# Attention with the softmax division moved behind the values: one scaling of the output per head pair

## The chip, the cores and the metric

The kernel runs on one core of a Trainium2 chip. The metric is the device time of one execution in microseconds (us). A core has TensorE (PE in the profile, its weight loads PEld), VectorE (DVE), ScalarE (ACT), GpSimd (POOL) and SyncE (SP, which issues DMAs). Matrix products are written to banks of PSUM; POOL works on SBUF alone here.

## What is computed

The reference is a network of two blocks with many layers. The change touches one layer of it, the attention of the second block. Queries, keys and values come from one projection; queries and keys are normalised and rotated; 16 query heads of 64 numbers share 4 heads of keys and values; 512 tokens attend to 512 tokens without a mask:

```python
def attend_block(q_blk):
    scores = jnp.einsum('bkgqd,bksd->bkgqs', q_blk, kt).astype(jnp.float32)
    p = jax.nn.softmax(scores, axis=-1).astype(vt.dtype)
    return jnp.einsum('bkgqs,bksd->bkgqd', p, vt)
...
return o @ w_o
```

The softmax divides each row of exponentials by its sum. As the values are multiplied from the right, that division may be made before or after the product with them.

## The kernel before, in words

All activations lie with the features on the partitions and the 512 tokens along the free side. Products with float32 accuracy are made of two parts: `split` (line 284) makes a rounded high part `h` by a cast on ACT (line 288) and the rest `l` by a subtraction on DVE (line 289), and `acc3` (line 326) issues three matmuls per pair of operands: high by high (line 330), one low part by high (331) and the other (333).

`attention` (line 1191) first makes queries, keys and values, then walks through 16 heads `n`, two of which share a 128-partition tile `tl = n // 2` (e = n % 2). It works on four blocks of 128 queries per head:

- `score(n, b)` (line 1323): two matmuls (1327, 1328) of a query block with all keys into a bank of the group `pj` (three banks, named pj and pk); the row maximum on DVE (1330); the exponential on ACT with the sum of the row as a second result (1332), into a block `P` of 128 queries x 512 keys; the reciprocal of the sum on DVE (1333); the block times that reciprocal on POOL (1334). There are eight buffers for `P`, which is two heads, and six for the small tile `st` that holds maximum, sum and reciprocal.
- `values(n, sb)` (line 1337), for each of four blocks of 128 keys: four transposes on TensorE (1342) bring the four query blocks' columns into one bank of the tag `ps` (three banks), `split` makes `pth` and `ptl` of it, and `acc3` adds their products with the values to the pair's bank `pa_o` (two banks). All four key blocks of a head read all four of its `P`.
- When both heads of a pair are done, `split` makes the high and low part of the pair's output, `xh_oa` and `xl_oa`, from the bank.
- `finish_q` (line 1269), once per pair for the first five pairs, prepares a later query tile: one matmul (1264) that spreads a norm, a product on DVE (1266), two casts on ACT (1273) and two subtractions on POOL (1274).
- `half_proj` (line 306) is the output projection. Its first half needs the outputs of the first four pairs, and it is written behind the last two pairs.

In the program the scores of head n+1 stand block by block ahead of the values of head n. The order in which the instructions stand in each engine's queue is not written by hand: the program is built with a scheduler that simulates the engines' times (`schedule_with_timeline_sim=True`), and the engines then take their queues in that order.

The helper `rotated` (line 1228) already spreads per-token numbers over partitions in the way that the change uses: a copy and a subtraction of a few columns into a zeroed operand `rh` (high and low part, 1254), four matmuls with the identity (1257) that turn it round, a copy to SBUF on ACT (1259), and in `unit` a matmul with a selecting matrix `selb` (1264).

Of the kernel before, what the change touches and what calls it, by code (L numbers as in the profile page):

```python
# [9 lines left out]
F32 = mybir.dt.float32  # L10
F32R = mybir.dt.float32r
ACTF = mybir.ActivationFunctionType
ALU = mybir.AluOpType
# [3 lines left out]
S = 512  # L17
# [213 lines left out]
class Net:  # L231
# [959 lines left out]
    def attention(self, pool, nrm):  # L1191
        nc, a = self.nc, self.a
# [8 lines left out]
        selb = pool.tile([128, 4, 128], F32R, name="selb", tag="selb")  # L1201
# [67 lines left out]
        def finish_q(rr, tl):  # L1269
            t = unit(rr, tl % 4, qm[:, tl, :])  # L1270
            for e in range(2):
                f, g = halves[e], halves[1 - e]
                nc.scalar.copy(qs[e][f, tl, :], t[f])
                nc.gpsimd.tensor_sub(qs[e][g, tl, :], t[f], qs[e][f, tl, :].bitcast(F32))
# [43 lines left out]
        rqs = (rq, rq2)  # L1318
        self.load_exp(rq2[0:16, 0:1].bitcast(F32))

        oa, probs, outs = {}, {}, {}

        def score(n, b):
            tl, e = n // 2, n % 2
            qb = slice(128 * b, 128 * b + 128)
            p = self.bank("pj")
            nc.tensor.matmul(p, qs[e][:, tl, qb], ks[e][:, tl // 4, :], start=True, stop=False)
            nc.tensor.matmul(p, qs[e][:, tl, qb], kl[e][:, tl // 4, :], start=False, stop=True)
            st = self.tmp("st", [128, 4], bufs=6)
            nc.vector.tensor_reduce(st[:, 0:1], p, axis=mybir.AxisListType.X, op=ALU.max, negate=True)  # L1330
            pr = pool.tile([128, S], F32, name=f"P{n}{b}", tag="P", bufs=8)
            nc.scalar.activation(pr, p, ACTF.Exp, bias=st[:, 0:1], accum_out=st[:, 1:2])
            nc.vector.reciprocal(st[:, 2:3], st[:, 1:2])
            nc.gpsimd.tensor_scalar(pr, pr, st[:, 2:3], None, ALU.mult)
            probs[n, b] = pr

        def values(n, sb):
            tl, e = n // 2, n % 2
            sk = slice(128 * sb, 128 * sb + 128)
            p = self.bank("pt")  # L1340
            for b in range(4):
                nc.tensor.transpose(p[:, 128 * b:128 * b + 128], probs[n, b][:, sk], ident)
            self.nt += 1
            th = pool.tile([128, S], F32R, name=f"pth{self.nt}", tag="pth", bufs=4)
            tw = pool.tile([128, S], F32R, name=f"ptl{self.nt}", tag="ptl", bufs=4)
            self.split(th, tw, p)
            if n % 2 == sb == 0:
                outs[tl] = self.ps.tile([128, S], F32, name=f"pa_o{tl}", tag="pa", bufs=2)
            vs = slice(64 * e, 64 * e + 128)
            self.acc3(outs[tl], [(vh[:, sb, tl // 4, vs], vl[:, sb, tl // 4, vs], th, tw)],  # L1350
                      e == sb == 0, e == 1 and sb == 3)

        for b in range(4):
            score(0, b)
            if b:
                value(b)
        for n in range(16):
            tl = n // 2
            for b in range(4):
                if n < 15:  # L1360
                    score(n + 1, b)
                values(n, b)
                if (n % 2, b) == (1, 1) and tl + 3 < KD:
                    finish_q(rqs[(tl + 3) // 4], tl + 3)
            if n == 10:
                self.unspill_x(xs)
            if n % 2:
                oa[tl] = self.pair(f"oa{tl}")
                self.split(*oa[tl], outs[tl])
                if tl > 5:  # L1370
                    self.half_proj(a["wo"], oa, 0, (2 * (tl - 6),))
        self.half_proj(a["wo"], oa, 0, (4, 6))
# [252 lines left out]
```

## Time and profile before

| | |
|---|---|
| median of 3 runs | 3715.67 us (3714.78 to 3716.51) |
| the profiled execution | 3715.35 us |
| its span, first to last instruction | 3713.6 us |
| busy share of PE, PEld, DVE, ACT, POOL | 98%, 79%, 56%, 37%, 22% |
| mean granted clock of TensorE | 0.990 of 2.4 GHz |
| mean busy share of the 16 DMA engines | about a third |

Times in the rows are us from the span's start. Durations in the lists by line or tile are in ns. A matmul's shown duration is longer than the time that it keeps TensorE from the next one, as matmuls are pipelined: the distance between the starts of two that follow each other is what one costs. In a list, "idle before" is the time that the engine stood still ahead of such instructions, with what ended it behind the arrow. A line can be that of a helper: L288 and L289 are the cast and the subtraction of `split`, L330, L331 and L333 the matmuls of `acc3`.

### The profile page before, as it was taken

How to read it: one execution, taken by the hardware profiler on the slowest of the kernel's cores; microseconds unless marked ns; L12 is line 12 of the kernel's file. 1: busy time of each engine (PE TensorE's matmuls, PEld its weight loads, DVE VectorE, ACT ScalarE, POOL GpSimd, SP SyncE). 2: the span in 40 equal slices, each digit the busy share in tenths (PEclk: the TensorE clock that was granted, in tenths of full speed). 3: DMA queues.
4: the chain of work that ended last, by engine and by line, in shares of the span. 5: the costliest groups of instructions: out<-in, count | busy, mean ns of one | idle time of the engine just before them, and what ended most of it. 6: DMA issues, size and time to landing. Idle time of an engine off the chain costs nothing.

```text
span 3713.6 us, 45381 instructions
## 1 busy us (share of the span) xinstructions
PE 3636.4 (98%) x17516; PEld 2945.8 (79%) x17516; DVE 2070.6 (56%) x3210; ACT 1368.3 (37%) x2031; POOL 826.8 (22%) x649
## 2 busy tenths in 40 slices
PE   8999999999999999999999999989999999899998
PEld 6878778978888878878888888767788888688886
DVE  4354585863334344467784345576656464866463
ACT  4223453142223223363233233265444343444342
POOL 2112121421011102220441012585101012401011
PEclk9999998999999999999999999999999999999999
DMA  4233434422323233434332333301432324323332
GB/s 138 89 109 104 151 114 122 132 85 89 98 90 116 88 99 111 155 97 128 120 139 96 95 105 97 120 18 53 147 105 92 96 93 132 116 64 93 94 95 81
DMA packets 180032, 386.84 MB, mean 104 GB/s; under 512 B 40742, under 2 KB 83750, under 8 KB 178792
## 3 DMA queue, kind: packets, MB, share of 16 engines
q1 hardware_dynamic: 179816, 383.95, 33.0%
q8 instruction: 137, 2.24, 0.3%
q14 instruction: 79, 0.65, 0.1%
HBM read 350.85 MB, written 33.03 MB: 103 GB/s over the span
## 4 chain that ended last, share of the span: by engine, by line
PE 88%; DVE 5%; issue 3%; DMA 2%; ACT 1%; POOL 1%; SPq 0%; DVEq 0%; ACTq 0%; POOLq 0%
PE pj L331 11%; PE pj L330 11%; PE pj L336 8%; PE pk L330 6%; PE pk L331 6%; PE ps L330 4%; PE pa L330 4%; PE ps L331 4%; PE pa L331 4%; PE ps L336 4%; PE pa L336 4%; PE pk L336 4%; PE pj L333 3%; PE pk L333 2%; DVE wl L289 1%
## 5 line engine op out<-in xcount | busy, mean ns | idle before, releaser
L288 ACT CAST wh<-wr 128x1024 fp32r<-128x1024 f32 x612 | 590.6, 965 | 1203.1 <-PE pj L331 485.9
L289 DVE TENSOR_TENSOR wl<-wr,wh 128x1024 fp32r<-128x1024 f32 x610 | 695.5, 1141 | 500.1 <-PE pj L336 128.7
L515 POOL TENSOR_TENSOR t<-s,u 128x512 f32<-128x512 f32 x88 | 176.7, 2009 | 1054.9 <-DVE u L514 955.6
L330 PE MATMUL pj<-xh_ffn_norm,wh 128*128 128x512 f32 x856 | 339.1, 396 | 0.0
L331 PE MATMUL pj<-xl_ffn_norm,wh 128*128 128x512 f32 x856 | 338.8, 396 | 0.0
L336 PE MATMUL pj<-xh_ffn_norm,wl 128*128 128x512 f32 x856 | 217.7, 396 | 0.0
L375 POOL TENSOR_TENSOR ssq<-ssq,c 128x512 f32<-128x512 f32 x76 | 112.6, 1481 | 434.2 <-ACT c L372 430.1
L330 PEld LDWEIGHTS pj<-xh_ffn_norm,wh 128*128 128x128 f32 x856 | 160.9, 188 | 39.1 <-ACT wh L288 0.8
L331 PEld LDWEIGHTS pj<-xl_ffn_norm,wh 128*128 128x128 f32 x856 | 160.7, 188 | 39.0 <-DVE xl_ffn_norm L292 0.3
L336 PEld LDWEIGHTS pj<-xh_ffn_norm,wl 128*128 128x128 f32 x856 | 160.5, 188 | 38.7
L330 PE MATMUL pk<-xh_ffn_norm,wh 128*128 128x512 f32 x472 | 187.1, 396 | 0.3 <-ACT wh L288 0.2
L331 PE MATMUL pk<-xl_ffn_norm,wh 128*128 128x512 f32 x472 | 186.9, 396 | 0.0
L553 POOL TENSOR_TENSOR t<-t,s 128x512 f32<-128x512 f32 x44 | 57.2, 1299 | 570.1 <-DVE s L572 501.0
L288 ACT CAST hh_ffn_norm<-t 128x512 fp32r<-128x512 f32 x132 | 81.4, 618 | 276.8 <-POOL t L515 273.5
L289 DVE TENSOR_TENSOR hl_ffn_norm<-t,hh_ffn_norm 128x512 fp32r<-128x512 f32 x132 | 93.8, 711 | 145.3 <-ACT hh_ffn_norm L288 145.0
L330 PE MATMUL pj<-hh_ffn_norm,wh 128*128 128x512 f32 x396 | 157.0, 397 | 0.0
L331 PE MATMUL pj<-hl_ffn_norm,wh 128*128 128x512 f32 x396 | 156.9, 396 | 0.0
L330 PE MATMUL ps<-xh_ffn_norm,wh 128*128 128x512 f32 x384 | 152.7, 398 | 0.0
L330 PE MATMUL pa<-xh_ffn_norm,wh 128*128 128x512 f32 x384 | 152.4, 397 | 0.0
L331 PE MATMUL ps<-xl_ffn_norm,wh 128*128 128x512 f32 x384 | 151.9, 396 | 0.0
L331 PE MATMUL pa<-xl_ffn_norm,wh 128*128 128x512 f32 x384 | 151.9, 396 | 0.0
L336 PE MATMUL pk<-xh_ffn_norm,wl 128*128 128x512 f32 x472 | 120.0, 396 | 0.0
(800 smaller groups left out, 8432.6 us busy)
## 6 DMA issues: line engine op xcount, KB each, us to landing
wr<-in_cu SPq DMA_DIRECT2D x88, 512.0 KB, 3.5
wr<-in_win SPq DMA_DIRECT2D x56, 512.0 KB, 3.5
wr<-in_ffn2g SPq DMA_DIRECT2D x44, 512.0 KB, 3.4
wr<-in_ffn2u SPq DMA_DIRECT2D x44, 512.0 KB, 3.4
wr<-in_ffn1g SPq DMA_DIRECT2D x43, 512.0 KB, 3.4
wr<-in_ffn1u SPq DMA_DIRECT2D x43, 512.0 KB, 3.5
wr<-in_ffn1d SPq DMA_DIRECT2D x32, 512.0 KB, 3.5
wr<-in_ffn2d SPq DMA_DIRECT2D x32, 512.0 KB, 3.5
```

The costliest lines, as they stand in the source:

```text
L288: nc.scalar.copy(h, src)
L289: lo.tensor_sub(l, src, h.bitcast(F32))
L330: mm(out, sh, mh, start=first and i == 0, stop=False)
L331: mm(out, sh, ml, start=False, stop=False)
L333: mm(out, sl, mh, start=False, stop=last and i == n - 1)
L336: mm(out, sl, mh, start=False, stop=last and i == n - 1)
L375: (nc.gpsimd if k < n - 1 else nc.vector).tensor_add(ssq, ssq, sq)
L515: nc.gpsimd.tensor_mul(t, s, u)
L553: nc.gpsimd.tensor_mul(t, t, cs[1])
```

## The change

The exponentials go unscaled through the transposes and the product with the values. The sums of a pair's two heads are gathered in one small tile. Once per pair, `shares` takes the reciprocals, spreads them over the 64 partitions of each head with the matmuls of the helper above, and the pair's output is multiplied by the result before it is split.

```diff
-        oa, probs, outs = {}, {}, {}
+        oa, probs, outs, sums = {}, {}, {}, {}
+        rn = self.tmp("ssq", [128, 4, 128], F32R, bufs=1)
+        nc.gpsimd.tensor_scalar(rn, self.ones[:, None, :].to_broadcast([128, 4, 128]), 0.0, None, ALU.mult)
...
+            if e == b == 0:
+                sums[tl] = self.tmp("sm", [128, 4, 2], bufs=3)
             st = self.tmp("st", [128, 4], bufs=6)
             nc.vector.tensor_reduce(st[:, 0:1], p, axis=mybir.AxisListType.X, op=ALU.max, negate=True)
             pr = pool.tile([128, S], F32, name=f"P{n}{b}", tag="P", bufs=8)
-            nc.scalar.activation(pr, p, ACTF.Exp, bias=st[:, 0:1], accum_out=st[:, 1:2])
-            nc.vector.reciprocal(st[:, 2:3], st[:, 1:2])
-            nc.gpsimd.tensor_scalar(pr, pr, st[:, 2:3], None, ALU.mult)
+            nc.scalar.activation(pr, p, ACTF.Exp, bias=st[:, 0:1], accum_out=sums[tl][:, b, e:e + 1])
             probs[n, b] = pr
+
+        def shares(tl):
+            w = self.tmp("sw", [128, 4, 2], bufs=2)
+            nc.vector.reciprocal(w, sums[tl])
+            nc.vector.tensor_copy(rn[:, :, 0:2], w)
+            nc.vector.tensor_sub(rn[:, :, 8:10], w, rn[:, :, 0:2].bitcast(F32))
+            p = self.bank("pt")
+            for b in range(4):
+                nc.tensor.matmul(p[:, 128 * b:128 * b + 128], rn[:, b], self.identr, start=True, stop=True)
+            rs = pool.tile([128, S], F32R, name=f"rn{tl}", tag="rs", bufs=2)
+            nc.scalar.copy(rs, p)
+            p = self.bank("pt")
+            nc.tensor.matmul(p, selb[:, 0, :], rs, start=True, stop=True)
+            w = self.tmp("a")
+            nc.scalar.copy(w, p)
+            return w
...
             if n % 2:
                 oa[tl] = self.pair(f"oa{tl}")
-                self.split(*oa[tl], outs[tl])
+                t = self.tmp("t")
+                nc.vector.tensor_mul(t, outs[tl], shares(tl))
+                self.split(*oa[tl], t)
```

The bank group `pt` is the tag `ps`, the three banks of the transposes. The tag `ssq` has one buffer, which the norms ahead of and behind the attention use for their sum of squares.

## Rows read from the trace of the kernel before

**Rows 1.** The page: busy us, share of the span and instructions of each engine.
```profile
PE 3636.4 (98%) x17516; PEld 2945.8 (79%) x17516; DVE 2070.6 (56%) x3210; ACT 1368.3 (37%) x2031; POOL 826.8 (22%) x649
```
**Rows 2.** ACT's timeline, output casts of pairs one and six: start, us, instruction, idle before.
```profile
2462.82 0.58 ACT L288 CAST xh_oa<-pa_o 128x512 fp32r<-128x512 f32 x1 [1.44 <-PE pa_o L333]
...
2543.70 0.58 ACT L288 CAST xh_oa<-pa_o 128x512 fp32r<-128x512 f32 x1
```
**Rows 3.** Instructions of tiles xh_oa, P and ssq: ns min/median/max, first and last start.
```profile
L330 PE MATMUL pj<-xh_oa,wh x33: 390/396/496, 2548.9 to 2598.8; 128*128 128x512 f32 x33
...
L288 ACT CAST xh_oa<-pa_o x8: 575/586/588, 2462.8 to 2590.2; 128x512 fp32r<-128x512 f32 x8
L289 DVE TENSOR_TENSOR xl_oa<-pa_o,xh_oa x8: 690/690/692, 2463.4 to 2590.9; 128x512 fp32r<-128x512 f32 x8
...
L1342 PE MATMUL ps<-mats,P x256: 270/272/330, 2442.3 to 2583.4; 128*128 128x128 f32 x128
...
L369 ACT ACTIVATE ssq<-x x1: 617/617/617, 2596.5 to 2596.5; 128x512 f32<-128x512 f32 x1
```
**Rows 4.** Two stretches: length, busy of PE, PEld, DVE, ACT, POOL; clock, DMA, GB/s.
```profile
2458.90:2540.10 81.20, 72.97 (x365) 53.58 (x366) 61.21 (x130) 56.95 (x134) 74.66 (x50) 1.00 0.07 27
2548.80:2596.00 47.20, 47.20 (x229) 38.39 (x228) 27.53 (x49) 20.08 (x41) 11.42 (x8) 1.00 0.18 56
```
**Rows 5.** POOL's timeline ahead of the loop and over one pair of it.
```profile
2438.86 6.60 POOL L1334 TENSOR_SCALAR P<-P,st 128x512 f32<-128x512 f32 x4 [5.92 <-DVE st L1333]
...
2489.49 2.65 POOL L1274 TENSOR_TENSOR qs<-t,qs 64x512 fp32r<-64x512 f32 x2
2492.23 6.18 POOL L1334 TENSOR_SCALAR P<-P,st 128x512 f32<-128x512 f32 x4
2499.72 6.19 POOL L1334 TENSOR_SCALAR P<-P,st 128x512 f32<-128x512 f32 x4 [1.30 <-DVE st L1333]
2505.99 2.65 POOL L1274 TENSOR_TENSOR qs<-t,qs 64x512 fp32r<-64x512 f32 x2
```
**Rows 6.** PE's timeline around the end of one head.
```profile
2498.34 0.60 PE L1342 MATMUL ps<-mats,P 128*128 128x128 f32 x4
...
2499.70 0.39 PE L333 MATMUL pa_o<-pth,vl 128*128 128x512 f32 x1
2499.93 0.40 PE L1327 MATMUL pj<-ks,qs 128*128 128x512 f32 x1
...
2500.85 0.38 PE L1342 MATMUL ps<-mats,P 128*128 128x128 f32 x2
```
**Rows 7.** Groups by line, 2458.9 to 2540.1: busy us, mean ns, idle before with releasers.
```profile
L331 PE MATMUL pa_o<-ptl,vh 128*128 128x512 f32 x41 | 19.1, 466 | 2.8 <-DVE ptl L289 2.6
L1332 ACT ACTIVATE P<-pj,st 128x512 f32<-128x512 f32 x27 | 18.6, 690 | 12.3 <-DVE st L1330 6.6 <-PE ps L1342 5.7
...
L330 PE MATMUL pa_o<-pth,vh 128*128 128x512 f32 x40 | 17.1, 427 | 5.1 <-ACT pth L288 5.1
...
L1333 DVE RECIPROCAL st<-st 128x1 f32<-128x1 f32 x41 | 6.7, 162 | 12.1 <-ACT P L1332 11.7
```
**Rows 8.** ACT's timeline: an exponential that waited for transposes.
```profile
2498.65 0.69 ACT L1332 ACTIVATE P<-pj,st 128x512 f32<-128x512 f32 x1 [0.94 <-PE ps L1342]
```
**Rows 9.** Instructions like the added ones, by line or tile: ns min/median/max, first and last start.
```profile
L406 DVE CAST rth<-rtok x17: 161/169/594, 30.2 to 3699.9; 128x4 fp32r<-128x4 f32 x16, 128x2 fp32r<-128x2 f32 x1
...
L1266 DVE TENSOR_TENSOR t<-ps,qm x8: 690/691/692, 2415.5 to 2518.7; 128x512 f32<-128x512 f32 x8
...
L1259 ACT CAST rs<-ps x3: 585/585/586, 2377.6 to 2435.4; 128x512 fp32r<-128x512 f32 x3
```
**Rows 10.** PE's timeline: the four turning matmuls of a norm.
```profile
2377.05 0.56 PE L1257 MATMUL ps<-identr,rh 128*128 128x128 f32 x4
```
**Rows 11.** The page's groups: cast and subtraction of the same shape with SBUF sources.
```profile
L288 ACT CAST hh_ffn_norm<-t 128x512 fp32r<-128x512 f32 x132 | 81.4, 618 | 276.8 <-POOL t L515 273.5
L289 DVE TENSOR_TENSOR hl_ffn_norm<-t,hh_ffn_norm 128x512 fp32r<-128x512 f32 x132 | 93.8, 711 | 145.3 <-ACT hh_ffn_norm L288 145.0
```

## The prediction

> **What bounds the kernel now.** I read the page's busy shares first, then the busy time of the stretch that the change touches, then one engine after another in it, and last who waits for whom. Over the whole span TensorE is busy nearly all the time [rows 1], so time can only be won where TensorE has holes. The attention loop has them. Its eight head pairs are marked by the eight casts of the finished output; the first and the sixth lie at 2462.82 and 2543.70 [rows 2], so a pair takes 80.88/5 = 16.2 us. From about 2548.9 the output projection begins to fill TensorE [rows 3], and until 2596 it is busy for 47.20 of 47.20 us [rows 4]. There a saving on any other engine buys nothing, and each added matmul costs its full time.
>
> In the five pairs from 2458.9 to 2540.1 POOL is the fullest engine: 74.66 of 81.2 us, 14.9 per pair (TensorE's 72.97 overlaps its matmuls with each other); DVE has 61.21 (12.2), ACT 56.95 (11.4) [rows 4]. POOL's 14.9 are eight products of a probability block at 6.18/4 = 1.55 us and two subtractions that split the next query tile, 2.65 together [rows 5]. It stops only for about 1 us per pair, when it waits for a reciprocal.
>
> TensorE issues 365 matmuls there, 73 per pair: 40 of scores and values, one that spreads a norm, and 32 transposes. Successive 512-column ones start 0.23 us apart (2499.70, 2499.93); four transposes show 0.60 us of which the last has 0.27, so each costs 0.11 [rows 6]. That is 41 x 0.23 + 32 x 0.11 = 12.95 us of work in 16.2, or 3.2 us of holes per pair. Of these the trace names 5.1 + 2.8 us in five pairs as TensorE waiting for the cast and the subtraction that split a transposed block [rows 7], 1.6 per pair.
>
> **What does not fit a plain POOL bound.** No instruction is listed as waiting for POOL's product. Its run of four that starts at 2492.23 ends at 2498.41 [rows 5], and the transposes that follow on TensorE are at 2498.34 and 2500.85 [rows 6]. The four at 2498.34 are the last of the head before, since the exponential at 2498.65 waited for them to free its block [rows 8]; so the products lay ready for 2.4 us. TensorE takes its queue in order, and that order is laid out when the program is built, with POOL's step in it. A new order is laid out without it.
>
> **The change, part by part.**
>
> *Removed.* 64 POOL products leave: 8 x 1.55 = 12.4 of POOL's 14.9 us per pair. The 1.55 us between an exponential and its transposes go as well, and so does the queue in which the fourth block of a head waited for the three before it, about 6.2 us in all [rows 5]. The 41 reciprocals of one column, 6.7 us in five pairs [rows 7], give DVE back 1.3 per pair. The small statistics tile is free after the exponential instead of after POOL; eight probability blocks still hold two heads, so an exponential still waits for the transposes two heads back, 5.7 us in the five pairs for the blocks scored in pj alone [rows 7, 8].
>
> *Added, once per pair.* DVE: a reciprocal, a copy and a subtraction of eight columns. The nearest rows are 0.162 for one column [rows 7] and 0.169 for four [rows 9]; I take 0.165 each, bounds 0.14 and 0.2, together 0.5. One product of a PSUM bank and a 128x512 tile takes 0.69 [rows 9]. DVE goes from 12.2 to 12.2 - 1.3 + 1.2 = 12.1. ACT: two copies out of PSUM at 0.585 [rows 9], from 11.4 to 12.6. TensorE: four 128-column matmuls and one of 512. The same four as they stand in the norms show 0.56 us of which I give the last 0.27 as for the transposes [rows 6, 10], so 0.10 each, and 4 x 0.10 + 0.23 = 0.63 per pair; 13.6 us of work instead of 12.95. The cast and subtraction of the output now read SBUF instead of PSUM: 0.618 against 0.586 and 0.711 against 0.690 on the same shape [rows 3, 11], 0.05 per pair, off TensorE's path.
>
> *Added, once.* The zero fill of the 128x512 operand on POOL, 1.55 us as the product of that shape, bounds 1.3 (half of 2.65, on half the partitions) and 1.65 (6.60/4); POOL stands idle for 5.92 us just ahead of the loop [rows 5]. Taken at nothing; without that cover it would delay what POOL does for the queries by at most 1.65. The operand's place is wanted again by the square at 2596.5 [rows 3], thirteen us after the last transposes at 2583.4: nothing. The last pair's output gets a product of 0.69 ahead of its cast; the cast was at 2590.2 [rows 3], while TensorE was full with the other half of the projection: nothing, at most 0.7.
>
> *Queues and banks.* Each pair takes two more turns of the three PSUM banks that the transposes use, eleven instead of nine, and the product waits on DVE for the spread sums. Behind it in DVE's queue stand the maxima of the next scores, for which the exponentials wait. The sums are complete one head before the product needs them, so all five steps can be done early. I take no stall, and keep the stall as a rival.
>
> *The sum.* Without POOL the floor of a pair is TensorE's 13.6. I don't take the floor: the 1.6 us in which TensorE waits for cast and subtraction do not involve POOL, and I keep them, so 13.6 + 1.6 = 15.2, a gain of 1.0 per pair. From the first transpose at 2442.3 to 2548.9 [rows 3] there are 106.6/16.2 = 6.6 pairs: -6.6 us. In the other 1.4 pairs TensorE is full: +1.4 x 0.63 = +0.9. Net -5.7. Behind the loop TensorE's work is unchanged and starts that much earlier. The profiled execution took 3715.35 us (span 3713.6 and 1.75 around it); the median of the runs, 3715.67, is 0.3 above. I put the sum on the median: **3710.0**. Bounds of the pair: 13.6 (no holes) and 16.2 (no gain).
>
> **The rivals.**
>
> *The forecast (0.45).* Waits for the split blocks between 1.0 and 2.2 us per pair: -9.7 to -1.8, so 3706 to 3714.
>
> *The floor (0.25).* POOL was what placed the holes, all of them, and the new order closes them: 2.6 x 6.6 = 17.2 less 0.9, 3699.4; with up to 1.0 us of holes left per pair it is 3699.4 to 3706. For it: POOL is 92% busy in the stretch [rows 4], and where TensorE had other work at hand from 2548.8 on, it had no holes at all. Against it: the waits on cast and subtraction, and three banks that must now also carry the sums. The Trainium skill, page "Perfetto Trace Analysis", section "Identifying the Most-Contended Engine", says that the engine of highest occupancy is the one to relieve, and that TensorE's room is judged by its weight loads, not its matmuls. By that rule POOL alone is the limit here and this rival is the outcome; the trace agrees on the occupancy (weight loads 53.58 of 81.2 us [rows 4]), but not on the waits, where no one waits for POOL.
>
> *POOL was beside the path (0.18).* The products lay ready for 2.4 us, the cycle is transposes, cast, subtraction, block free, exponential, and the pair stays at 16.2 with the new work inside its holes. Only the full stretch pays: +0.9, 3716.6. This is the case in which the change does what it says and the time doesn't follow.
>
> *Slower: the spread sums stall TensorE (0.12).* The 512-column matmul of each pair stands in TensorE's queue behind the ACT copy of the four before it. If the order puts the two next to each other, TensorE waits at least that copy, 0.585, in every pair; with no gain elsewhere that is 8 x (0.63 + 0.585) = +9.7, 3725.4. It decides if the stall exceeds the 1.0 gained per pair. For it: the order is made with estimated durations, and DVE, ACT and TensorE alternate in five steps. Against it: the steps can start a head early, and the norms run the same pattern with the two matmuls apart.
>
> **How the numbers follow.** The forecast and the two cases with no or full gain carry 0.88. A range from 3700 to 3720 takes in the forecast, nearly all of the floor case, POOL beside the path, and the milder part of the stalls; about 0.15 is left out. The forecast's own range is 3706 to 3714. 0.2% of the time, about what a measurement of this kernel can tell from no change, is 7.4 us: faster means below 3708.2. The floor case gives 0.25 and a third of the forecast 0.15, so 0.40 faster; the rest of the forecast (0.30) and POOL beside the path (0.18) make 0.48 the same; the stalls 0.12 slower.
>
> **What the profile would show.** POOL should fall from 74.7 us to about 13 in five pairs; DVE stay at 12.1 per pair; ACT rise to 12.6; the distance between output casts be 15.2 in place of 16.2; matmuls per pair be 78. TensorE's waits for cast and subtraction should stay near 1.6 per pair: near zero means the floor case. Output casts still 16.2 apart mean POOL beside the path. A wait of the spreading matmul for an ACT copy, or of the product for one, in every pair means the stall. I am wrong in the mechanism if the pair shrinks while those waits grow, or if the time moves in stretches behind 2600 or ahead of 2440, where no work changes.

## The result, and the profile after

The changed kernel took **3692.86 us** (median of 4 runs, 3687.6 to 3693.97) against 3715.52 for the kernel before on the same chip (3714.78 to 3716.51): a ratio of 0.9934 [0.9923, 0.9946], or -22.7 us. The forecast was 3710.0, with a range down to 3700. The gain is four times the one forecast, so the question is where the other three quarters come from. The profiled execution took 3693.65 us, with a span of 3691.8.

The page's busy shares answer to [rows 1]. POOL has lost 95 us and TensorE only 9, of a span that is 22 shorter:

```profile
PE 3627.7 (98%) x17556; PEld 2952.2 (80%) x17556; DVE 2066.6 (56%) x3178; ACT 1375.5 (37%) x2047; POOL 732.1 (20%) x586
```

**The loop came out nearly as forecast.** ACT's timeline of the kernel after, the output casts of pairs one, two, five and six (to [rows 2]):

```profile
2452.63 0.69 ACT L288 CAST xh_oa<-t 128x512 fp32r<-128x512 f32 x1
2468.65 0.62 ACT L288 CAST xh_oa<-t 128x512 fp32r<-128x512 f32 x1
...
2514.37 0.62 ACT L288 CAST xh_oa<-t 128x512 fp32r<-128x512 f32 x1
2528.06 0.63 ACT L288 CAST xh_oa<-t 128x512 fp32r<-128x512 f32 x1
```

From the first to the sixth a pair takes 75.43/5 = 15.1 us, between the second and the fifth 45.72/3 = 15.24; forecast was 15.2, down from 16.2. The busy time of those three middle pairs and of the full stretch behind the loop, of the kernel after (length, busy of PE, PEld, DVE, ACT and POOL with their instructions, clock, DMA share, GB/s; to [rows 4]):

```profile
2468.65:2514.37 45.72, 44.45 (x236) 33.72 (x235) 36.71 (x67) 36.85 (x89) 7.67 (x6) 1.00 0.13 47
2532.40:2578.00 45.60, 45.60 (x225) 37.43 (x224) 28.04 (x47) 21.50 (x43) 0.00 (x0) 1.00 0.18 58
```

Per pair that is DVE 12.2 (forecast 12.1), ACT 12.3 (12.6) and POOL 2.6 (2.6). TensorE has 78 matmuls per pair; the 236 of the row include two at its edges. Behind the loop TensorE is still full.

**But most of the time moved where no work changed.** Four starts cut the span into stretches: the first projection of this layer, the first transposes of the loop, the first half of the output projection, the first projection of the next layer. The lists by tile of the kernel after (ns min/median/max, first and last start):

```profile
L330 PE MATMUL pj<-xh_attn_norm,wh x56: 389/395/498, 2329.9 to 2400.8; 128*128 128x512 f32 x56
...
L1360 PE MATMUL ps<-mats,P x256: 270/272/273, 2433.1 to 2560.9; 128*128 128x128 f32 x128
...
L330 PE MATMUL pj<-xh_oa,wh x40: 392/396/482, 2532.4 to 2590.3; 128*128 128x512 f32 x40
...
L330 PE MATMUL pj<-xh_xattn_norm,wh x72: 395/395/628, 2620.2 to 3227.9; 128*128 128x512 f32 x72
```

The two of them that [rows 3] lacks, of the kernel before:

```profile
L330 PE MATMUL pj<-xh_attn_norm,wh x56: 392/395/497, 2339.4 to 2410.2; 128*128 128x512 f32 x56
...
L330 PE MATMUL pj<-xh_xattn_norm,wh x72: 392/395/477, 2636.5 to 3246.5; 128*128 128x512 f32 x72
```

| stretch of the profiled execution, us | before | after | difference |
|---|---|---|---|
| start to the first transposes of the loop | 2442.3 | 2433.1 | -9.2 |
| to the first output projection | 106.6 | 99.3 | -7.3 |
| to the next layer's projection | 87.6 | 87.8 | +0.2 |
| to the end of the span | 1077.1 | 1071.6 | -5.5 |

The layer's own first matmul already starts 9.5 us earlier, 2329.9 against 2339.4, while the engines' queues up to there hold the same instructions in the same order, but for one: POOL's zero fill of 2.46 us. What differs is the pace of one kind of matmul. The lists by tile of `hl_ffn_norm`, an operand of the down-projections of all feed-forward layers, first of the kernel before, then of the kernel after:

```profile
L331 PE MATMUL pj<-hl_ffn_norm,wh x396: 388/397/402, 141.8 to 3678.4; 128*128 128x512 f32 x198
...
L331 PE MATMUL ps<-hl_ffn_norm,wh x264: 392/394/400, 149.6 to 3686.1; 128*128 128x512 f32 x132
...
L331 PE MATMUL pa<-hl_ffn_norm,wh x264: 391/394/400, 157.3 to 3693.8; 128*128 128x512 f32 x132
```

```profile
L331 PE MATMUL pj<-hl_ffn_norm,wh x396: 387/392/403, 141.5 to 3657.2; 128*128 128x512 f32 x198
...
L331 PE MATMUL ps<-hl_ffn_norm,wh x264: 387/389/399, 149.1 to 3664.7; 128*128 128x512 f32 x132
...
L331 PE MATMUL pa<-hl_ffn_norm,wh x264: 388/389/399, 156.6 to 3672.1; 128*128 128x512 f32 x132
```

The first product into `pj`, `ps` and `pa` are each 33 matmuls apart (11 blocks of features, three matmuls per block). So 66 matmuls take 157.3 - 141.8 = 15.5 us before, 0.235 each, and 156.6 - 141.5 = 15.1 after, 0.229 each. Taken over all starts that follow without a gap, a down-projection's 264 matmuls follow each other at 234.3 ns before and 229.0 after in six of the twelve stretches, at 233.4 and 226.8 in four, and at 233.3 and 233.4 in two. That is 6 x 264 x 5.3 + 4 x 264 x 6.6 ns = 8.4 + 7.0 = 15.4 us. The six and the two lie ahead of the attention, where 9.2 went, the four behind it, where 5.5 went; single executions differ by a few us in either. With the 7.1 of loop and output projection it makes 22.5 of the measured 22.7.

What can change the pace of a matmul whose queue is the same? The change's two new small tiles, `sm` (three buffers of 32 bytes per partition) and `sw` (two), belong to a pool of temporaries that stands for the whole program, and the tiles allocated behind that pool's space lie 160 bytes higher on every partition. In the built program `hh` and `hl` moved by that much; the weights `wh` and `wl` and the up-projections' operands `xh` and `xl` did not. (A matmul call of the program names its weights and, behind them, a second operand, called the moving operand below.)

### The profile page after: what moved, and what is told of

The parts are those of the page before. It is cut to its first block, busy times and chain, and to the rows that moved or that the text cites. A ratio compares the mean times of both kernels' runs of the same rounds, so it can differ in the third digit from the quotient of the medians.

```text
span 3691.8 us, 45267 instructions
## 1 busy us (share of the span) xinstructions
PE 3627.7 (98%) x17556; PEld 2952.2 (80%) x17556; DVE 2066.6 (56%) x3178; ACT 1375.5 (37%) x2047; POOL 732.1 (20%) x586
## 4 chain that ended last, share of the span: by engine, by line
PE 76%; DVE 4%; issue 3%; DMA 2%; POOL 1%; ACT 1%; SPq 0%; DVEq 0%; ACTq 0%; POOLq 0%
PE pj L331 10%; PE pj L330 10%; PE pj L336 7%; PE pk L330 5%; PE pk L331 5%; PE pa L330 4%; PE ps L330 4%; PE pa L331 4%; PE ps L331 4%; PE ps L336 3%; PE pa L336 3%; PE pk L336 3%; PE pj L333 3%; PE pk L333 2%; PE pj L725 1%
```

## The experiments

**The move alone (e1), and the change without the move (e2).** In e1 the kernel before gets the two tags and nothing else; in e2 the changed kernel takes its small tiles from tags that exist already:

```diff
 oa, probs, outs = {}, {}, {}
+nc.gpsimd.memset(self.tmp("sm", [128, 4, 2], bufs=3), 0.0)
+nc.gpsimd.memset(self.tmp("sw", [128, 4, 2], bufs=2), 0.0)
```
```diff
-sums[tl] = self.tmp("sm", [128, 4, 2], bufs=3)
+sums[tl] = self.tmp("rtok", [128, 4, 2], bufs=4)
-w = self.tmp("sw", [128, 4, 2], bufs=2)
+w = self.tmp("rv", [128, 4, 2], bufs=2)
```

> The kernel before with two zeroed small tiles of the change's sizes (three of 32 bytes, two of 32) and nothing else, so that every tile of the later pools starts 160 bytes higher, as after the change. Layout theory: the matmuls with the hidden activations hh and hl start 229.0 instead of 233.8 ns apart, about 3168 of them, so -15 us: 3700 to 3702, and the attention loop keeps its 16.2 us per pair. Rival (the gain came from the work that left, and the earlier start of the attention was that run's own): 3715.5, spacing 233.8.

> The change with its two small tiles put into buffers that exist already (the norms' 32-byte tiles), so that no other tile moves; the queues are those of the change. Layout theory: the loop's gain alone, -7 us: 3708 to 3709.5, pairs of 15.2 us, hh and hl matmuls 233.8 ns apart, attention starting when it did before. Rival: as the change, 3692.9.

e1 took 3700.26 us, a ratio of 0.996 [0.9945, 0.9975] to 3714.85 before: -14.6 us. e2 took 3706.3, 0.998 [0.9971, 0.999]: -8.6. The two add up to -23.1, against -22.7 of the change. The list by tile of e1, with TensorE's queue unchanged and two fills of 0.1 us on POOL added, shows the pace of the kernel after (66 matmuls in 157.9 - 142.8 = 15.1 us):

```profile
L331 PE MATMUL pj<-hl_ffn_norm,wh x396: 387/392/402, 142.8 to 3667.0; 128*128 128x512 f32 x198
...
L331 PE MATMUL ps<-hl_ffn_norm,wh x264: 387/389/399, 150.3 to 3674.4; 128*128 128x512 f32 x132
...
L331 PE MATMUL pa<-hl_ffn_norm,wh x264: 387/389/399, 157.9 to 3681.9; 128*128 128x512 f32 x132
```

In e2 the spacing is that of the kernel before, 66 matmuls in 155.6 - 140.1 = 15.5 us:

```profile
L331 PE MATMUL pj<-hl_ffn_norm,wh x396: 388/397/403, 140.1 to 3665.4; 128*128 128x512 f32 x198
...
L331 PE MATMUL pa<-hl_ffn_norm,wh x264: 391/394/400, 155.6 to 3680.8; 128*128 128x512 f32 x132
```

Its loop is that of the kernel after: the middle pairs are 15.24 us apart, and from the first transposes to the output projection it takes 99.4 us. So **the change as it was meant is worth -8.6 us, and two thirds of the measured gain is a side effect of where its tiles lie.** The profiled execution of e2 was the fastest of ten, 3701.88, and 5.7 us ahead of the kernel before by the time the loop begins, at an unchanged pace of matmuls. Of these, 1.7 arise ahead of the first down-projection, where the clock granted to TensorE over the first 40 us was 0.96 of 2.4 GHz in the kernel before and 1.00 in e2; the rest stays open. Over e2's ten runs the mean granted clock was 0.9906, over the 25 of the kernel before 0.9897, so a part of the 8.6 may be the clock's. From the first transposes to the end of the span e2's profile is 7.8 us shorter, which leaves the division into two thirds and one third as it is.

**What about the place matters (e3, e4, e5)?** e3 moves all tiles, weights and operands, by 32 bytes; e4 moves weights, `hh` and `hl` by 32 and leaves `xh` and `xl`; e5 moves the same tiles as e4 by 224. In all three the engines' queues are those of the kernel before.

```diff
-self.pick = res.tile([128, 7], F32, name="pick")
+self.pick = res.tile([128, 15], F32, name="pick")
```
```diff
-self.rmt = self.res.tile([128, 2], F32, name="rmt", tag="rmt")
+self.rmt = self.res.tile([128, 10], F32, name="rmt", tag="rmt")[:, 0:2]
```
```diff
-self.rmt = self.res.tile([128, 2], F32, name="rmt", tag="rmt")
+self.rmt = self.res.tile([128, 64], F32, name="rmt", tag="rmt")[:, 0:2]
```

> The kernel before with one resident tile 32 bytes wider: activations xh and xl, weights wh and wl, and hh and hl all start 32 bytes higher; queues unchanged. If the start of the moving operand decides (fast at an odd multiple of 32 bytes): all 512-column matmuls at about 229 ns, some 14000 of them by 4.5 ns, -60 us: 3655. If the moving operand must lie like the weights (both even or both odd multiples of 32 bytes): xh and wh still differ, and hh and wh too, 3715.5, no change. If neither: hh alone fast, -15 us, 3700.

> The kernel before with the last resident tile ahead of the weight pool 32 bytes wider: weights and hh, hl start 32 bytes higher, xh and xl stay; queues unchanged. If the start of the moving operand decides: hh and hl fast, -15 us, 3700. If moving operand and weights must lie alike: xh and xl, now alike with the weights, fast, some 11000 matmuls by 4.5 ns, -50 us: 3666, and hh unchanged at 233.8.

> The kernel before with the last resident tile ahead of the weight pool 224 bytes wider: weights and hh, hl start 224 bytes higher, xh and xl stay; queues unchanged. Theory that the distance of the moving operand's start from the weights' start, taken modulo 256 bytes, sets the pace (seen so far: 0 gives 226.8 ns, 64 gives 229.0, 96 to 224 give 233.3 to 234.3): xh and xl come to distance 0, so their matmuls go from 233.3 to 226.8 ns, some 9000 by 6.5 ns, -58 us: 3657; hh and hl keep their distance and their 233.4 to 234.3. Rival (the moving operand's own place decides, xh has not moved): xh unchanged at 233.3, 3715.

e3 took 3714.7 us and e4 3714.51, both 1.0 [0.999, 1.0009]: no change, and no spacing moved. So it is not the start of the operand by itself. e5 took **3666.15**, 0.9866 [0.9851, 0.9881]: -49 us, without one instruction changed. The busy time of a stretch of up-projections (60 to 120 us) and one of down-projections (145 to 190), columns as above, of the kernel before and of e5:

```profile
60.00:120.00 60.00, 60.00 (x259) 48.32 (x258) 22.27 (x26) 17.84 (x21) 10.56 (x5) 1.00 0.29 97
145.00:190.00 45.00, 45.00 (x194) 36.17 (x193) 14.80 (x19) 9.39 (x12) 0.00 (x0) 1.00 0.32 91
```

```profile
60.00:120.00 60.00, 60.00 (x266) 49.69 (x266) 23.54 (x27) 17.85 (x21) 12.32 (x6) 1.00 0.29 97
145.00:190.00 45.00, 45.00 (x193) 36.16 (x192) 14.10 (x18) 9.07 (x12) 0.00 (x0) 1.00 0.33 97
```

The granted clock is 1.00 in all four, and TensorE is busy throughout; but e5 gets 266 matmuls into the 60 us in which the kernel before gets 259. What fits all places of the projections seen so far is the distance from the start of the weights to the start of the moving operand, as a remainder of 256 bytes. The starts are those that the built programs list per partition, the spacing is the mean distance of successive starts:

| matmuls | before | after | e5 | e9 (below) |
|---|---|---|---|---|
| `hh`, `hl`: six stretches | 160 B: 234.3 ns | 64 B: 229.0 ns | 160 B: 234.3 ns | 0: 226.9 ns |
| `hh`, `hl`: two stretches | 192 B: 233.3 ns | 96 B: 233.4 ns | 192 B: 233.3 ns | 0: 226.7 ns |
| `hh`, `hl`: four stretches | 96 B: 233.4 ns | 0: 226.8 ns | 96 B: 233.4 ns | 0: 226.7 ns |
| `xh`, `xl`: up-projections | 224 B: 233.3 ns | 224 B: 233.3 ns | 0: 226.9 ns | 0: 226.9 ns |

e4 adds a fifth: `xh` at 192 stayed at 233.3. Distances of 32 and 128 were not tried. A difference of 256 bytes doesn't matter: in e9 `xh` lies at 256 and `hh` at 0 as a remainder of 512, at the same pace.

The traces hold two more kinds of 128x512 matmuls, counted where starts lie less than 245 ns apart. The products of the memory (96 in each of two layers, with `wh` and `wl` as the moving operand) lie at 64 and 96 in the kernel before and follow each other at 229.7 and 233.6 ns; after the change they lie at 160 and 192, with 234.2 and 233.3. They bear the rule out. The attention's own products lie at 0 in every kernel here, as do those of the attentions behind it, but they follow each other at 231.5 and 230.1 ns in the kernel before. They stand in short runs among other work; what keeps them above 226.9 is not shown.

The expectation for e5 was 58 us. The 6,200 recorded up-projection matmuls at 6.4 ns less are 40 us; the 1,290 of the mixing layers went from 233.1 to only 227.6, 7 us more, and the other projections make it 55 by the same count. As 49 were measured, not all of the faster pace reaches the time.

**The change with the better places (e6, e9).** e6 is the changed kernel with e5's edit. e9 adds to it one tile ahead of `hh` in the pools of the gated layers, the ones not yet at 0, so that all these operands lie at a distance of 0:

```diff
+gap = 160 if gain == "ffn2_norm1" else 192
+nc.gpsimd.memset(pool.tile([128, gap // 4], F32, name=f"gap_{gain}", tag="gap"), 0.0)
```

> The change with the same tile 224 bytes wider: xh at distance 0 from the weights, hh and hl at the change's distances 64, 0, 96 and 0. Distance theory: -58 us on top of the change, 3635, faster than both kernels; xh at 226.8 ns and hh as in the change. Rival: as the change, 3693.

> The kernel of e6 with one more tile ahead of hh in each feed-forward pool (160 bytes wide, 192 in the pools of the layer that already stood at 224 bytes from its weights), zero-filled once by POOL, so that the distance from the start of hh to the start of its weights is a multiple of 256 in all segments, as it is for xh since e6. If this distance sets the pace of the matmuls: the down-projections of the layers that stand at 229.0 ns go to 226.8 and those of the one layer that stands at 233.4 go there too, some 1580 matmuls x 2.2 ns + 530 x 6.6 ns = 7 us less than e6: 3637. If the pace follows an address of the operand itself and only happened to be good at the places tried so far: spacings of these matmuls that differ from 226.8 somewhere, and 3644 or more.

e6 took 3644.37 us, 0.9807 [0.9793, 0.9822], and e9 **3634.94**, 0.9784 [0.9767, 0.98], 80.2 below the kernel before on its chip and better than both kernels. The stretches of e9, against those of the kernel before above:

```profile
60.00:120.00 60.00, 60.00 (x266) 49.71 (x265) 23.54 (x27) 18.43 (x22) 12.67 (x6) 1.00 0.30 97
145.00:190.00 45.00, 45.00 (x200) 37.27 (x199) 14.30 (x18) 9.55 (x13) 0.00 (x0) 1.00 0.33 97
```

Now the down-projections have it too, 200 matmuls against 194. The rule foretold 3637, the rival of e9 (an address of the operand itself) 3644 or more. The places account for 1,580 x 2.2 ns + 528 x 6.6 ns = 7.0 of the 9.4 us by which e9 is below e6; TensorE's queue is that of e6, and POOL has the four added fills; the other 2.4 us stay open. Why the distance matters no run here shows. As e5 and the change are worth 49 and 23 and e6 is 71 below its kernel before, the two gains add up.

**What POOL's step was worth (e7, e8).** e7 is the kernel before without the reciprocals and the products on POOL (lines 1333 and 1334); it leaves the division out and adds nothing, and no tile moves. e8 is e2 with a POOL step of the old size put back at its old place.

```diff
-nc.vector.reciprocal(st[:, 2:3], st[:, 1:2])
-nc.gpsimd.tensor_scalar(pr, pr, st[:, 2:3], None, ALU.mult)
```
```diff
+nc.gpsimd.tensor_scalar(pr, pr, self.ones[:, 0:1], None, ALU.mult)
 probs[n, b] = pr
```

> The kernel before without the reciprocals and without POOL's product: the division is left out, nothing stands in for it, and no tile moves. Loop theory (POOL's step set the order and the pace of the loop): a pair falls from 16.2 to about 14.5 (15.2 less the 0.63 of TensorE's added matmuls), -10 us, 3704.5, two below the change without the shift. Rival (POOL beside the path, its result lay ready 2.4 us early): pairs of 16.2, 3715.

> The change without the shift, but with POOL's product over each block kept (by a column of ones, so the numbers stay): the spread sums are paid and POOL's step stays in the path. Loop theory: pairs of 16.2 or more, 3715 to 3720, the 8 us of the unshifted change gone. Rival (the gain came from the reciprocals and the statistics tile that is free earlier): as the unshifted change, 3706.

e7 took 3698.49 us, 0.9953 [0.9938, 0.9968]: -17 us. e8 took 3728.22, 1.0035 [1.0023, 1.0048]: +12.7. ACT's timeline, the casts of pairs two and five, of e7 and then of e8:

```profile
2475.86 0.59 ACT L288 CAST xh_oa<-pa_o 128x512 fp32r<-128x512 f32 x1
...
2518.75 0.59 ACT L288 CAST xh_oa<-pa_o 128x512 fp32r<-128x512 f32 x1 [0.20 <-PE pa_o L333]
```

```profile
2478.66 0.62 ACT L288 CAST xh_oa<-t 128x512 fp32r<-128x512 f32 x1 [1.15 <-DVE t L1389]
...
2534.59 0.62 ACT L288 CAST xh_oa<-t 128x512 fp32r<-128x512 f32 x1 [1.14 <-DVE t L1389]
```

A pair takes 14.3 us without the step, and 18.6 with the step and the shares together, against 16.2 expected. The kernel before has 16.3 between the same two casts. So POOL's step sets the pace of the loop, though no instruction waited for it by name; e7 takes DVE's reciprocals away with it, but e8 puts only the POOL step back, and is 21.9 us above e2. Whether it does so by its time or by the order that the program is built with for it is not shown: in the built programs some 600 places of TensorE's queue hold another matmul in e7 than in the kernel before, and in e8 than in e2. In e8 the waits grow that the kernel before already had (its middle three pairs, groups by line: busy us, mean ns, idle before):

```profile
L1361 PE MATMUL ps<-mats,P 128*128 128x128 f32 x98 | 16.0, 280 | 1.8 <-DVE t L1266 1.8
...
L331 PE MATMUL pa_o<-ptl,vh 128*128 128x512 f32 x24 | 11.7, 487 | 2.4 <-DVE ptl L289 2.4
...
L330 PE MATMUL pa_o<-pth,vh 128*128 128x512 f32 x24 | 10.5, 437 | 4.6 <-ACT pth L288 4.6
```

The waits for cast and subtraction are 7.0 us in three pairs, 2.3 per pair, where the kernel before had 1.6 [rows 7]; the transposes' wait for DVE is 0.6 per pair. With the 0.63 of the shares' own matmuls that names 1.9 of the 2.4 us between 16.2 and 18.6; the rest has no wait of its own. The price of the shares themselves is the difference of e2 and e7: 3706.3 - 3698.49 = 7.8 us, or 8.4 with each taken against the kernel before on its own chip.

## Why the prediction was wrong, point by point

- **The step that failed: "Behind the loop TensorE's work is unchanged and starts that much earlier."** The same was taken silently for everything ahead of the loop. The instructions are unchanged, but their pace is not: 3,168 matmuls in the down-projections took 15.4 us less, because new tiles moved their operands. The sum had no term for this. The prediction did name the sign by which to know it, "if the time moves in stretches behind 2600 or ahead of 2440, where no work changes", and that is what the table of stretches shows. Nothing in the rows gave its size: of the four kinds of matmuls in the table, the kernel before runs none at a distance of 0 or 64. The hints in its trace were that it runs the same shape at 233.3, 233.4 and 234.3 ns, and the memory's products of one layer, at 64, at 229.7.
- **The loop was right.** Without the move the change gives -8.6 us (interval of the ratio: -10.8 to -3.7) against a forecast of -5.7 with its own range of -9.7 to -1.8. The loop of the profiled execution went from 106.6 to 99.3 us, -7.3 against -6.6. In the full stretch behind it the shares of the last 1.4 pairs were to cost +0.9; it shows +0.2.
- **The size of the holes was right, their cause was not.** The sum kept 1.6 us per pair as waits for cast and subtraction, and 15.24 less 13.6 of work leaves 1.6. But the waits it meant have all but gone, and TensorE now waits for free score banks, that is for the exponentials that read them. Groups by line of the middle three pairs, of the kernel before and then of the kernel after:

```profile
L331 PEld LDWEIGHTS pa_o<-ptl,vh 128*128 128x128 f32 x24 | 4.5, 188 | 4.6 <-DVE ptl L289 4.1
L330 PEld LDWEIGHTS pa_o<-pth,vh 128*128 128x128 f32 x24 | 4.5, 187 | 5.6 <-ACT pth L288 4.9
```

```profile
L331 PE MATMUL pa_o<-ptl,vh 128*128 128x512 f32 x24 | 10.3, 430 | 0.0
L330 PE MATMUL pa_o<-pth,vh 128*128 128x512 f32 x24 | 10.1, 421 | 0.0
...
L1329 PE MATMUL pj<-ks,qs 128*128 128x512 f32 x16 | 7.4, 461 | 0.8 <-ACT P L1336 0.8
...
L330 PEld LDWEIGHTS pa_o<-pth,vh 128*128 128x128 f32 x24 | 4.5, 189 | 1.1 <-ACT pth L288 0.5
...
L331 PEld LDWEIGHTS pa_o<-ptl,vh 128*128 128x128 f32 x24 | 4.5, 188 | 1.1 <-DVE ptl L289 0.6
...
L1329 PEld LDWEIGHTS pj<-ks,qs 128*128 128x128 f32 x16 | 3.0, 188 | 3.3 <-ACT P L1336 2.3 <-issue 0.9
...
L1348 ACT CAST rn<-ps 128x512 fp32r<-128x512 f32 x3 | 1.8, 613 | 0.0
...
L1329 PEld LDWEIGHTS pk<-ks,qs 128*128 128x128 f32 x8 | 1.5, 188 | 1.7 <-ACT P L1336 1.1 <-issue 0.4
...
L1341 DVE RECIPROCAL sw<-sm 128x8 f32<-128x8 f32 x3 | 0.6, 192 | 0.0
...
L1350 PEld LDWEIGHTS ps<-rn,selb 128*128 128x128 f32 x3 | 0.6, 186 | 0.9 <-ACT rn L1348 0.9
```

- On the weight loads the waits for cast and subtraction were 9.0 us in three pairs before, 3.0 per pair and so nearly all of the 3.2 us of holes; the prediction read 1.6 on the matmuls alone. They are 1.1 us in three pairs after, 0.4 per pair. The waits for exponentials are 3.4 there, 1.1 per pair. Waits for the split blocks near zero were to mean the floor case. They did not, since a new wait took their place. e7, which has neither POOL's step nor the shares, comes nearest to it: 14.3 us per pair, against 12.95 of work.
- **The two halves of the sum were both mis-sized, and offset each other.** Taking POOL's step and DVE's reciprocals away is worth 17 us (e7), not the 1.6 to 1.7 per pair over 6.6 pairs, 11, that the sum implies before the shares; the shares cost 7.8 us, not 8 x 0.63 = 5. The single durations were near: reciprocal 0.192 us (taken as 0.165, within 0.14 to 0.2), the ACT copy 0.613 (0.585).
- **The zero fill was outside its bounds, and free.** POOL's timeline of the kernel after; bounds were 1.3 to 1.65 us. It ran 122 us ahead of the first transposes and not just before them, and the next POOL work waited 14.8 us for something else. Two fills of the same form, shape and type (line 1218, of `rh`) take 1.48 us each in the same profile, inside the bounds; why this one took longer is open.

```profile
2311.08 2.46 POOL L1323 TENSOR_SCALAR ssq<-ones 128x512 fp32r<-128x512 f32 x1 [1.62 <-PE pa L452]
2328.38 1.84 POOL L466 TENSOR_TENSOR x<-x,r 128x512 f32<-128x512 f32 x1 [14.84 <-ACT r L416]
```

- **The rivals.** POOL beside the path fell with e7 and e8. The stalling spread matmul is there, as the last row above shows, but with 0.9 us in three pairs, 0.3 per pair, and not the 0.585 in each that would have decided. The floor was not reached. The rule weighed with it, that the engine of highest occupancy is the one to relieve (the Trainium skill, page "Perfetto Trace Analysis", section "Identifying the Most-Contended Engine"), named POOL, and e7 agrees: -17 us. The prediction's objection to it, that no one waits for POOL by name, was no evidence; but the rule did not give the size either, as the pair stopped at 15.24 and not at 13.6.

## What to carry to other kernels

A change that allocates anything can move tiles it never mentions; compare the starts of the operands of the busiest matmuls before and after, and the spacing of matmul starts in stretches the change doesn't touch, before giving a gain to the change. An edit that fixes the places (here by taking existing tags) separates the two in one run. And an engine that is full in a stretch can set its pace without one listed wait, by its time or by the order in which the others' queues were laid out with it: take the work away once to price it. Here no run tells whether its time or that order did it.

## What was not expected of the hardware

The spacing of successive 128x512 matmuls with fp32r operands depended, in the feed-forward stretches, on where the moving operand lies against the weights: 226.7 to 226.9 ns where the distance is a multiple of 256 bytes, 229.0 at 64, and 233.3 to 234.3 at 96, 160, 192 and 224, at the same granted clock of 1.00 and with the same queues (e1, e5). In a kernel in which TensorE is full, that alone was worth 49 us of 3715 for one operand (e5), and with the change and the other operand 80 (e9). The busy share doesn't show it: TensorE is busy for 60.00 of 60.00 us at either pace.
